# Block products of one group accumulated in shared PSUM banks, in the MLP's first product

## Chip, cores and metric

One Trainium2 chip, one of its cores. The metric is the device time of one launch, in microseconds (us). Smaller is better.

## What is computed

Two transformer blocks after each other on 1024 tokens of 1024 features, in fp32. Each block is x + mixer(norm(x)), then x + MLP(norm(x)). The mixers differ (a gated scan; a convolution beside a retention), the MLP is the same in both:

```
def sq_relu_mlp(u, w_up, w_down):
    hdn = jax.nn.relu(u @ w_up)          # [1024, 1024] @ [1024, 4096]
    return (hdn * hdn) @ w_down          # [1024, 4096] @ [4096, 1024]
```

The change is in the first of the two products, which runs once in each of the two MLPs.

## The kernel before

A fp32 product is made of three matmuls on fp32r parts: each operand is split into a high part (a ScalarE cast) and a low part (a VectorE subtraction), and `mm3` adds high x high, high x low and low x high in PSUM. An instruction's operands are printed here as moving operand first, then weights.

The MLP's products go by blocks of two by two, with seven block products in place of eight (Winograd's form). With A of the weights and B of the tokens:

```
S1 = A21 + A22, S2 = S1 - A11, S3 = A11 - A21, S4 = A12 - S2
T1 = B12 - B11, T2 = B22 - T1, T3 = B22 - B12, T4 = B21 - T2
U2 = A11 B11 + S2 T2, U3 = U2 + S3 T3
C11 = A11 B11 + A12 B21, C12 = U2 + S1 T1 + S4 B22, C21 = U3 + A22 T4, C22 = U3 + S1 T1
```

P1 is A11 B11, P2 A12 B21, P3 S4 B22, P4 A22 T4, P5 S1 T1, P6 S2 T2, P7 S3 T3. One **group** is these seven products for 256 hidden features: each is 12 matmuls (4 tiles of the contracted half, 3 parts) into a [128, 512] tile, which fills one PSUM bank. The first product of an MLP has 16 groups (0 to 15 below). The four blocks C11 (emitted as row 0, half 0), C12 (0, 1), C22 (1, 1) and C21 (1, 0) then pass max with 0 and the norm's factor `rb` (VectorE, L1155) and a square (ScalarE, L1156), and go to DRAM as blocks of the second product. Features of groups 14 and 15 are also cast and stored split (L1117, L1120).

PSUM has two pools of four banks, `acc` (called `accb()`) and `ps2` (called `bank()`). Each product takes a fresh bank. VectorE and ScalarE add up and evacuate as the products end: per group one ScalarE copy (P1, L1166) and seven VectorE additions (L1152 four times, L1173, L1175, L1179).

Order of work: each engine runs its own instructions strictly as the program emits them, and waits on semaphores for the others. Everything beside the products is planned by hand in ticks. A tick comes after each product: `tick()` first emits what is planned for this point, and only then come the copies and additions of the product just issued. Planned for the ticks are loads, the sums and splits of the next group's weight blocks (`W1_AT = (0, 3, 4, 4, 4, 4)`: full blocks at tick 0, f sums at 3, the rest at 4; L787 casts, L788 subtractions, L819 to L825 sums of which GpSimd does one), and in the last groups the splits of hidden features for the second product (L180, L181).

Group 0 is special. The last tile of its tokens is made just before it (`project`, L972 to L1000), its T sums and splits are still running while its first products run, and the norm's statistics are folded in: `rest` (split of T3, T4) at tick 0, two times eight tiny matmuls L291 (`stats_a`, `stats_b`) at ticks 2 and 3, a chain of small VectorE instructions for the root (L246 to L252), spread and turned by matmuls L305 at tick 5, and copied to `rb` by ScalarE (L1018).

Of the kernel before, what the change touches and what calls it, by code (L numbers as in the profile page):

```python
# [35 lines left out]
# Ticks (two a product of eight) between a product and each step of the side work that is planned with it.  # L36
# [17 lines left out]
# The engine of each sum of blocks: V VectorE, G GpSimd.  # L54
# [7 lines left out]
# The order of the hidden eighths (but the last) in the second product; the first eighth's parts that are stored split.  # L62
# [5 lines left out]
# columns of the small per-feature constants  # L68
# [6 lines left out]
class Slots:  # L75
    """Equal SBUF tiles of [128, 1024] words, handed out and taken back as the program is emitted."""
# [21 lines left out]
class Kernel:  # L98
# [85 lines left out]
    def use(self, n=1):  # L184
        """The next n weight slabs; loads and splits run ahead of them."""
# [15 lines left out]
    def mm3(self, ps, ah, al, bh, bl, start, stop):  # L201
        mm = self.nc.tensor.matmul
        mm(ps, lhsT=ah, rhs=bh, start=start, stop=False)  # L203
        mm(ps, lhsT=ah, rhs=bl, start=False, stop=False)  # L204
        mm(ps, lhsT=al, rhs=bh, start=False, stop=stop)  # L205

    def unit(self, w, src, half):
        """One tile of outputs [128 columns of w, 512 tokens]."""
# [12 lines left out]
    def unit_b(self, ws, src, pair, ps=None):  # L221
        """Two token tiles times 256 columns of w: [128 tokens, 2, 256]."""
        if ps is None:
            ps = self.accb()
        for j in range(2):
            self.col_b(ws, src, 2 * pair + j, range(KT), ps[:, j * 256:(j + 1) * 256])
            self.tick()
        return ps
# [10 lines left out]
    def rsqrt(self, ss, n, scale, square=False, engine=None):  # L239
        """(scale * ss + eps) ** -0.5 of a small [128, n] tile, by Newton steps."""  # L240
# [20 lines left out]
    def square_in(self, xt, j, half, sqs, gain=1.0, engine=None, late=False):  # L261
        """Adds the squares of a feature tile to the running sums."""
# [22 lines left out]
    def stats(self, sqs, chunks, ps=None):  # L285
        """Sums over the features of each token of some chunks: [128 tokens, chunks]."""
# [7 lines left out]
    def spread(self, z, n):  # L294
        """[128 tokens, n] -> n diagonal matrices of 128 tokens."""
# [6 lines left out]
    def turn(self, b, n=4):  # L302
        """n diagonal matrices of 128 tokens -> PSUM [128 equal rows, 128 n tokens]."""
# [19 lines left out]
    def hgrn_scan(self, h, qf, kr, f, v):  # L323
        """Scores within a chunk by levels: blocks of one token to blocks of 64, each with the blocks after it."""
# [7 lines left out]
        def small(ps, rhs, n):  # L332
            """Keys of each 32 tokens against n of these tokens' queries: [tokens, chunks, n]."""
# [10 lines left out]
        # Two levels at once, groups of four blocks of b tokens with totals D0 to D3:  # L344
        # queries of blocks 1, 2, 3 against the block before; D1 q2, D2 q3; D1 D2 q3.
# [142 lines left out]
    def transpose7(self, src, dst, scale):  # L488
        """Per chunk [features, tokens] -> [tokens, features], all chunks but the last."""
# [12 lines left out]
    def states7(self, kt, v, s, decay):  # L502
        """s[:, c] = the state before chunk c."""
# [16 lines left out]
    def outputs(self, a3, v, qx, s):  # L520
        """Per chunk [tokens, head features]: within the chunk, and from the state before it."""
# [66 lines left out]
    def values(self, ps, pair, vs, zs):  # L588
        """[128 tokens, 2, 256] -> two heads' values, scaled per token."""
# [1129 lines left out]
```

## Time and profile before

| | |
|---|---|
| time, median of 3 runs | 2275.82 us (2274.45 to 2278.04) |
| profiled execution, first to last instruction (the span; all that the profile gives of its own time) | 2272.1 us |
| TensorE matmul busy | 2236.2 us, 98% |
| VectorE busy | 1753.2 us, 77% |
| ScalarE busy | 879.4 us, 39% |
| GpSimd busy | 404.6 us, 18% |

PE is TensorE's matmuls, DVE is VectorE, ACT ScalarE, POOL GpSimd. Matmuls are pipelined, so one's duration (0.39 us) overlaps the next; what counts is the distance of their starts, 0.227 us for 512 columns.

### The profile page before, as it was taken

The page shows a single profiled execution, that of the slowest core. Times are in us where ns is not written, and L with a number is a line of the kernel's source. Part 1 is how long each engine was busy: PE and PEld are TensorE (multiplying, and loading weights), DVE is VectorE, ACT ScalarE, POOL GpSimd, SP SyncE. Part 2 cuts the span into 40 slices and gives each one's busy share as a digit, 9 for nine tenths or more (in the row PEclk, how much of TensorE's full clock was granted, in tenths as well). Part 3 has the DMA queues.
Part 4 walks back from the last instruction along what each step waited for, and adds up shares of the span by engine and source line. Part 5 has one row for each costly group of instructions (what it writes and reads, how often), then busy time and mean ns, then how long its engine had stood idle before and what let it go on. Part 6 is the DMA issues. An engine that isn't in the chain of part 4 may idle for free.

```text
span 2272.1 us, 32892 instructions
## 1 busy us (share of the span) xinstructions
PE 2236.2 (98%) x13102; PEld 1882.1 (83%) x13102; DVE 1753.2 (77%) x2593; ACT 879.4 (39%) x1346; POOL 404.6 (18%) x381
## 2 busy tenths in 40 slices
PE   8999999999999999999999999999999999999998
PEld 7888887888888888888889888887888888888887
DVE  6756658636888888989996556885698888889996
ACT  6334433434433335434344242224533334533322
POOL 0122212101111111222210011013111111122223
PEclk9999999999999999999999999999999999999999
DMA  5001010123344448444512011112234446744442
GB/s 181 30 29 38 21 38 30 47 74 130 118 170 160 151 167 300 152 154 149 195 46 103 28 38 38 47 38 75 89 137 165 161 152 209 261 153 147 160 158 75
DMA packets 80219, 261.91 MB, mean 115 GB/s; under 512 B 8897, under 2 KB 11457, under 8 KB 80065
## 3 DMA queue, kind: packets, MB, share of 16 engines
q1 hardware_dynamic: 79488, 259.28, 33.1%
q8 instruction: 103, 1.69, 0.3%
q10 hardware_dynamic: 576, 0.52, 0.1%
q14 instruction: 52, 0.42, 0.1%
HBM read 186.37 MB, written 73.40 MB: 114 GB/s over the span
## 4 chain that ended last, share of the span: by engine, by line
PE 86%; DVE 11%; ACT 1%; issue 1%; DMA 1%; SPq 0%; DVEq 0%; ACTq 0%
PE acc L203 20%; PE acc L204 20%; PE acc L205 20%; PE ps L203 7%; PE ps L205 7%; PE ps L204 7%; PE ps L530 1%; PE ps L532 1%; PE ps L510 1%; DVE ac L386 1%; DVE r L358 1%; DVE r L355 1%; PE ps L305 1%; PE ps L560 0%; DVE lo L174 0%
## 5 line engine op out<-in xcount | busy, mean ns | idle before, releaser
L203 PE MATMUL acc<-hi,hi 128*128 128x512 f32 (+1 forms) x824 | 315.1, 382 | 1.2 <-ACT acc L1213 1.1
L204 PE MATMUL acc<-lo,hi 128*128 128x512 f32 (+1 forms) x824 | 313.9, 381 | 0.8 <-POOL lo L1484 0.8
L205 PE MATMUL acc<-hi,lo 128*128 128x512 f32 (+1 forms) x824 | 313.8, 381 | 0.0
L203 PE MATMUL acc<-uh,hi 128*128 128x512 f32 x768 | 306.2, 399 | 0.0
L204 PE MATMUL acc<-ul,hi 128*128 128x512 f32 x768 | 300.0, 391 | 0.0
L205 PE MATMUL acc<-uh,lo 128*128 128x512 f32 x768 | 299.9, 391 | 0.0
L203 PE MATMUL ps<-hi,hi 128*128 128x512 f32 x712 | 277.2, 389 | 0.0
L205 PE MATMUL ps<-hi,lo 128*128 128x512 f32 x712 | 277.0, 389 | 0.0
L204 PE MATMUL ps<-lo,hi 128*128 128x512 f32 x712 | 277.0, 389 | 0.0
L1156 ACT ACTIVATE hq<-hq 128x512 f32<-128x512 f32 x128 | 81.0, 633 | 338.0 <-DVE hq L1155 270.8
L203 PEld LDWEIGHTS acc<-hi,hi 128*128 128x128 f32 x824 | 154.9, 188 | 32.3 <-ACT acc L1213 2.0
L204 PEld LDWEIGHTS acc<-lo,hi 128*128 128x128 f32 x824 | 154.9, 188 | 31.0 <-POOL lo L1484 1.2
L205 PEld LDWEIGHTS acc<-hi,lo 128*128 128x128 f32 x824 | 154.9, 188 | 29.7
L205 PEld LDWEIGHTS acc<-uh,lo 128*128 128x128 f32 x768 | 144.6, 188 | 30.8
L203 PEld LDWEIGHTS acc<-uh,hi 128*128 128x128 f32 x768 | 144.5, 188 | 30.4 <-ACT v L595 0.2
L204 PEld LDWEIGHTS acc<-ul,hi 128*128 128x128 f32 x768 | 144.7, 188 | 28.9 <-issue 0.5
L205 PEld LDWEIGHTS ps<-hi,lo 128*128 128x128 f32 x712 | 133.6, 188 | 27.8
L204 PEld LDWEIGHTS ps<-lo,hi 128*128 128x128 f32 x712 | 133.6, 188 | 27.7
L203 PEld LDWEIGHTS ps<-hi,hi 128*128 128x128 f32 x712 | 133.6, 188 | 27.7
L180 ACT CAST hi<-h 128x1024 fp32r<-128x1024 f32 x96 | 100.2, 1053 | 134.8 <-DVE lo L181 76.5
L181 DVE TENSOR_TENSOR lo<-h,hi 128x1024 fp32r<-128x1024 f32 x96 | 121.9, 1277 | 6.5 <-ACT hi L180 6.5
L174 DVE TENSOR_TENSOR lo<-w,hi 128x1024 fp32r<-128x1024 f32 x70 | 85.0, 1221 | 49.5 <-ACT hi L173 49.5
(271 smaller groups left out, 4696.0 us busy)
## 6 DMA issues: line engine op xcount, KB each, us to landing
w<-in_w SPq DMA_DIRECT2D x202, 512.0 KB, 4.5
hf<-f SPq DMA_DIRECT2D x28, 512.0 KB, 2.6
hfull<-hq SPq DMA_DIRECT2D x28, 512.0 KB, 3.5
hg<-g SPq DMA_DIRECT2D x28, 512.0 KB, 4.0
h<-hfull SPq DMA_DIRECT2D x28, 512.0 KB, 3.8
h<-hf SPq DMA_DIRECT2D x28, 512.0 KB, 4.5
h<-hg SPq DMA_DIRECT2D x28, 512.0 KB, 3.5
xs<-x SPq DMA_DIRECT2D x16, 512.0 KB, 2.7
```

The costliest lines, as they stand in the source:

```text
L174: self.low.tensor_tensor(lo, st, hi.bitcast(F32), op=SUB)
L180: self.nc.scalar.copy(hi, src)
L181: self.low.tensor_tensor(lo, src, hi.bitcast(F32), op=SUB)
L203: mm(ps, lhsT=ah, rhs=bh, start=start, stop=False)
L204: mm(ps, lhsT=ah, rhs=bl, start=False, stop=False)
L205: mm(ps, lhsT=al, rhs=bh, start=False, stop=stop)
L305: self.nc.tensor.matmul(ps[:, :n * P], lhsT=self.cs[:, C_ONES:C_ONES + P], rhs=b[:, :n * P], start=True, stop=True)
L355: ve.tensor_tensor(rv[:, 0:3], qv[:, 1:4], dv[:, 1:4], op=MUL)
L358: ve.tensor_tensor(rv[:, 3:5], rv[:, 1:3], dv[:, 1:3].to_broadcast([P, 2, n, b]), op=MUL)
L386: ve.copy_predicated(av[:, j:], mask[:, v0:v1], pv[:, v0:v1])
L510: nc.tensor.matmul(ps[:, c * P:(c + 1) * P], lhsT=kt[:, t], rhs=v[:, t], start=True, stop=True)
L1156: nc.scalar.activation(t, t, AF.Square)
```

## The change

The first product of both MLPs calls `chain` in place of `group`; the second product still calls `group`. The order of the products becomes P1, P2, P6, P5, P7, P3, P4, and three banks serve a group. P1, P6, P7 and P4 all go into bank x, so that it holds P1, then U2, then U3, then C21. P5 and P3 go into bank y, P2 into bank z. After P1, P6, P5 and P7 ScalarE copies the sum out (`keep`). VectorE adds three pairs (C11, C22 from two copies, C12), and C21 is read from PSUM by the max instruction itself.

```
-    def mm3(self, ps, ah, al, bh, bl, start, stop):
+    def mm3(self, ps, ah, al, bh, bl, start, stop, more=False):
         mm = self.nc.tensor.matmul
-        mm(ps, lhsT=ah, rhs=bh, start=start, stop=False)
+        mm(ps, lhsT=ah, rhs=bh, start=start, stop=False, skip_group_check=more)
...
+    CHAIN = ("P1", "P2", "P6", "P5", "P7", "P3", "P4")
+    CHAIN_BANK = {"P1": "x", "P2": "z", "P6": "x", "P5": "y", "P7": "x", "P3": "y", "P4": "x"}
+    CHAIN_W_FREE = {"P2": ("k_full",), "P5": ("k_f",), "P3": ("k_g",), "P4": ("k_one",)}
+    CHAIN_B_FREE = {"P1": ("k_one",), "P3": ("k_full",), "P5": ("k_f",), "P4": ("k_g",)}
+    def chain(self, w, bs, emit, free, own=False):
+        banks, kept = {}, {}
+        def keep(name, ps):
+            t = kept[name] = self.tmp()
+            self.nc.scalar.copy(t, ps)
+        for name in self.CHAIN:
+            an, bn = self.PARTS[name]
+            b = self.CHAIN_BANK[name]
+            fresh = b not in banks
+            if fresh:
+                banks[b] = self.accb() if b == "x" or own else self.bank()
+            ps = banks[b]
+            ah, al = w[an]
+            for k, blocks in enumerate(bs):
+                c = slice(k * P, (k + 1) * P)
+                bh, bl = blocks[bn]
+                self.mm3(ps, ah[:, c], al[:, c], bh, bl, fresh and k == 0, k == len(bs) - 1,
+                         not fresh)
...
+            self.tick()
+            if name in ("P1", "P6", "P5", "P7"):
+                keep(name, ps)
+            if name == "P2":
+                emit(0, 0, ps, kept["P1"])
+            elif name == "P7":
+                emit(1, 1, kept["P7"], kept["P5"])
+            elif name == "P3":
+                emit(0, 1, ps, kept["P6"])
+            elif name == "P4":
+                emit(1, 0, ps, None)
...
-                elif (r, h) == (1, 1):
+                elif (r, h) == (0, 1):
                     self.at(HIDDEN_AT[0], first)
...
-                t = st[r][:, tk]
-                v.tensor_tensor(t, ps, other, op=ADD)
+                t = src = st[r][:, tk]
+                if other is None:
+                    src = ps
+                else:
+                    v.tensor_tensor(t, ps, other, op=ADD)
                 def finish():
-                    v.scalar_tensor_tensor(t, t, 0.0, rb[:, tk], op0=MAX, op1=MUL)
+                    v.scalar_tensor_tensor(t, src, 0.0, rb[:, tk], op0=MAX, op1=MUL)
...
-            def out(name, ps):
-                if name == "P1":
-                    st["p1"] = self.tmp()
-                    nc.scalar.copy(st["p1"], ps)
...
-                elif name == "P6":
-                    u2 = st["u2"] = self.tmp()
-                    v.tensor_tensor(u2, ps, st["p1"], op=ADD)
-                    t = self.tmp()
-                    v.tensor_tensor(t, st["P5"], u2, op=ADD)
-                    emit(0, 1, st["P3"], t)
-                elif name == "P7":
-                    u3 = st["u3"] = self.tmp()
-                    v.tensor_tensor(u3, ps, st["u2"], op=ADD)
-                    emit(1, 1, st["P5"], u3)
...
-            self.group(w, us, 0, hidden(i), free, ("P2", "P5", "P7") if i else ("P5", "P7"))
+            self.chain(w, us, hidden(i), free, i == 0)
```

TensorE in group 0 of the first MLP, where the second product (P2, bank acc_6100) ends and the third begins. Before, the third is P3, in a bank of its own:

```order
L205 MATMUL acc_6100<-hi_5835,lo_5967 128x512
L203 MATMUL acc_6100<-hi_5979,hi_5966 128x512
L204 MATMUL acc_6100<-lo_5980,hi_5966 128x512
L205 MATMUL acc_6100<-hi_5979,lo_5967 128x512
L203 MATMUL acc_6115<-hi_5517,hi_5988 128x512
L204 MATMUL acc_6115<-lo_5518,hi_5988 128x512
L205 MATMUL acc_6115<-hi_5517,lo_5989 128x512
L203 MATMUL acc_6115<-hi_5676,hi_5988 128x512
```

Of the change, at the same place, the third is P6, in bank acc_6073, in which P1 stands:

```order
L206 MATMUL acc_6100<-hi_5835,lo_5967 128x512
L204 MATMUL acc_6100<-hi_5979,hi_5966 128x512
L205 MATMUL acc_6100<-lo_5980,hi_5966 128x512
L206 MATMUL acc_6100<-hi_5979,lo_5967 128x512
L204 MATMUL acc_6073<-hi_5539,hi_5997 128x512
L205 MATMUL acc_6073<-lo_5540,hi_5997 128x512
L206 MATMUL acc_6073<-hi_5539,lo_5998 128x512
L204 MATMUL acc_6073<-hi_5698,hi_5997 128x512
```

The bank of the third product moved from a fresh one to P1's.

ScalarE in the same group, from the cast of T1 and T2's last tile (f_5983) to the copy of `rb`. Before (g_6001 holds T3 and T4, w_6090 the next group's weights, acc_6073 is P1):

```order
L787 CAST hi_6005<-f_5983 128x1024
L787 CAST hl_6009<-w_5814 128x512
L787 CAST hi_6086<-g_6001 128x1024
L787 CAST hi_6094<-w_6090 128x1024
L1166 COPY tmp_6098<-acc_6073 128x512
L787 CAST hl_6187<-w_6092 128x512
L787 CAST hi_6190<-f_6168 128x1024
L787 CAST hi_6194<-g_6184 128x1024
L1018 COPY rb_6012<-ps_6220 128x512
L1018 COPY rb_6012<-ps_6223 128x512
L1156 ACTIVATE hq_6113<-hq_6113 128x512 x2
```

Of the change (the copies L914 are, in order, of P1, P6, P5 and P7):

```order
L788 CAST hi_6005<-f_5983 128x1024
L788 CAST hl_6009<-w_5814 128x512
L788 CAST hi_6086<-g_6001 128x1024
L788 CAST hi_6094<-w_6090 128x1024
L914 COPY tmp_6098<-acc_6073 128x512
L914 COPY tmp_6132<-acc_6073 128x512
L914 COPY tmp_6172<-acc_6134 128x512
L788 CAST hl_6189<-w_6092 128x512
L788 CAST hi_6192<-f_6169 128x1024
L788 CAST hi_6196<-g_6186 128x1024
L914 COPY tmp_6204<-acc_6073 128x512
L1063 COPY rb_6012<-ps_6220 128x512
```

P1's copy kept its place behind the four casts; the copies of P6 and P5 came in behind it, and that of P7 behind the three casts of the next weights and ahead of `rb`.

ScalarE in group 15 of the first MLP, from the first block's square on. Before (h are hidden features for the second product, w, f and g its weights):

```order
L1156 ACTIVATE hq_8414<-hq_8414 128x512
L1117 CAST tmp_8418<-hq_8414 128x512
L787 CAST hl_8440<-w_8299 128x512
L180 CAST hi_8456<-h_8263 128x1024
L180 CAST hi_8460<-h_8281 128x1024
L180 CAST hi_8485<-h_8374 128x1024
L180 CAST hi_8489<-h_8376 128x1024
L787 CAST hi_8493<-f_8385 128x1024
L787 CAST hi_8497<-g_8437 128x1024
L1156 ACTIVATE hq_8414<-hq_8414 128x512
```

Of the change (the copies are of P6, P5 and P7):

```order
L1204 ACTIVATE hq_8339<-hq_8339 128x512
L1162 CAST tmp_8343<-hq_8339 128x512
L788 CAST hl_8364<-w_8231 128x512
L914 COPY tmp_8367<-acc_8286 128x512
L180 CAST hi_8382<-h_8194 128x1024
L180 CAST hi_8386<-h_8213 128x1024
L914 COPY tmp_8398<-ps_8369 128x512
L180 CAST hi_8412<-h_8299 128x1024
L180 CAST hi_8416<-h_8301 128x1024
L788 CAST hi_8420<-f_8310 128x1024
L788 CAST hi_8424<-g_8361 128x1024
L914 COPY tmp_8435<-acc_8286 128x512
```

Three copies came in between the casts, that of P7 behind all of them.

## Rows read from the trace of the kernel before

**Rows 1.** The page's head and its first part: busy time, share of the span and number of instructions of each engine.

```profile
span 2272.1 us, 32892 instructions
PE 2236.2 (98%) x13102; PEld 1882.1 (83%) x13102; DVE 1753.2 (77%) x2593; ACT 879.4 (39%) x1346; POOL 404.6 (18%) x381
```

**Rows 2.** What TensorE waited for in the whole span: us in total, times, longest. The first is in the first block's mixer, the second at the two ends of the MLPs' first products.

```profile
PE ps L381 <- DVE r L359: 17.0, 19, 2.3
...
PE acc L203 <- ACT acc L1213: 1.1, 2, 0.9
```

**Rows 3.** Busy time of the engines in groups 1 to 14 of the first and of the second MLP.

```profile
core 0: us, PE busy (x) PEld busy (x) DVE busy (x) ACT busy (x) POOL busy (x), PEclk, DMA share, GB/s
596.00:862.00 266.00, 266.00 (x1175) 220.25 (x1174) 227.35 (x306) 94.81 (x134) 40.78 (x28) 1.00 0.46 162
1658.00:1924.00 266.00, 266.00 (x1176) 220.24 (x1175) 227.23 (x307) 94.94 (x134) 40.77 (x28) 1.00 0.46 162
```

**Rows 4.** TensorE in order of time, group 0 of the first MLP (start, duration): last matmul of the second product, first of the third, eight statistics matmuls, first matmul of the fourth, the other eight, first matmul of P4.

```profile
578.64 0.39 PE L205 MATMUL acc<-hi,lo 128*128 128x512 f32 x1
578.87 0.39 PE L203 MATMUL acc<-hi,hi 128*128 128x512 f32 x1
...
581.59 0.94 PE L291 MATMUL ps<-cs,sqs 128*128 128x1 f32 x8
582.39 0.49 PE L203 MATMUL ps<-hi,hi 128*128 128x512 f32 x1
...
585.26 0.95 PE L291 MATMUL ps<-cs,sqs 128*128 128x1 f32 x8
...
592.97 0.79 PE L203 MATMUL acc<-hi,hl 128*128 128x512 f32 x1
```

**Rows 5.** ScalarE in order of time in the same group: cast of T3 and T4, of the next weights, the copy of P1, and later the first copy to `rb` (two in one row). In brackets idle time before, and what ended it.

```profile
582.54 1.06 ACT L787 CAST hi<-g 128x1024 fp32r<-128x1024 f32 x1 [0.77 <-DVE g L849]
583.50 1.04 ACT L787 CAST hi<-w 128x1024 fp32r<-128x1024 f32 x1
584.44 0.58 ACT L1166 COPY tmp<-acc 128x512 f32<-128x512 f32 x1
...
595.47 1.06 ACT L1018 COPY rb<-ps 128x512 f32<-128x512 f32 x2
```

**Rows 6.** VectorE in order of time in the same group: the addition of C11, and the first of the small instructions for the root.

```profile
587.11 0.68 DVE L1152 TENSOR_TENSOR hq<-acc,tmp 128x512 f32<-128x512 f32 x1
587.71 0.15 DVE L246 TENSOR_SCALAR ms<-ps 128x8 f32<-128x8 f32 x1
```

**Rows 7.** Group 0 of the second MLP: first matmul of the third product, and the copy of P1.

```profile
1641.06 0.39 PE L203 MATMUL acc<-hi,hi 128*128 128x512 f32 x1
...
1646.64 0.57 ACT L1166 COPY tmp<-acc 128x512 f32<-128x512 f32 x1
```

**Rows 8.** Two stretches of the first block's mixer, columns as in rows 3; PEclk is the granted clock of TensorE as a share of 2.4 GHz.

```profile
390.00:395.60 5.60, 2.37 (x74) 1.88 (x72) 5.43 (x16) 1.02 (x2) 0.00 (x0) 1.00 0.00 0
395.60:399.20 3.60, 3.60 (x19) 2.83 (x10) 2.79 (x8) 1.62 (x4) 2.25 (x2) 0.53 0.02 5
```

**Rows 9.** Group 8 of the first MLP in order of time: its first matmul; ScalarE's cast of full weights and copy of P1; VectorE's addition of C11; ScalarE's square and its casts of f and g.

```profile
729.41 0.39 PE L203 MATMUL acc<-hl,hi 128*128 128x512 f32 x1
...
732.55 0.57 ACT L1166 COPY tmp<-acc 128x512 f32<-128x512 f32 x1
...
735.12 0.69 DVE L1152 TENSOR_TENSOR hq<-ps,tmp 128x512 f32<-128x512 f32 x1 [1.15 <-PE ps L205]
...
736.62 0.63 ACT L1156 ACTIVATE hq<-hq 128x512 f32<-128x512 f32 x1 [3.50 <-issue]
...
738.92 1.05 ACT L787 CAST hi<-f 128x1024 fp32r<-128x1024 f32 x1 [1.16 <-POOL f L820]
739.87 1.05 ACT L787 CAST hi<-g 128x1024 fp32r<-128x1024 f32 x1
```

**Rows 10.** Group 15 of the first MLP in order of time: its first matmul; on ScalarE the square of group 14's last block, then of this group's first block, the casts.

```profile
862.69 0.39 PE L203 MATMUL acc<-hl,hi 128*128 128x512 f32 x1
...
864.34 0.63 ACT L1156 ACTIVATE hq<-hq 128x512 f32<-128x512 f32 x1 [0.65 <-DVE hq L1155]
...
872.54 0.63 ACT L1156 ACTIVATE hq<-hq 128x512 f32<-128x512 f32 x1 [3.58 <-DVE hq L1155]
...
873.74 0.62 ACT L787 CAST hl<-w 128x512 fp32r<-128x512 f32 x1
874.26 3.89 ACT L180 CAST hi<-h 128x1024 fp32r<-128x1024 f32 x4
878.05 1.05 ACT L787 CAST hi<-f 128x1024 fp32r<-128x1024 f32 x1
879.01 1.04 ACT L787 CAST hi<-g 128x1024 fp32r<-128x1024 f32 x1
```

**Rows 11.** After group 15: the matmul of the second product that waited for ScalarE's copy L1213, in the first and in the second MLP.

```profile
892.32 0.50 PE L203 MATMUL acc<-hi,hi 128*128 128x512 f32 x1 [0.91 <-ACT acc L1213]
...
1953.83 0.50 PE L203 MATMUL acc<-hi,hi 128*128 128x512 f32 x1 [0.22 <-ACT acc L1213]
```

**Rows 12.** Groups of equal instructions over the whole span (busy us, mean ns of one, idle before): the first copy and two of the additions of the groups, 32 groups in all.

```profile
L1175 DVE TENSOR_TENSOR tmp<-ps,tmp 128x512 f32<-128x512 f32 x32 | 22.1, 691 | 1.1
L1173 DVE TENSOR_TENSOR tmp<-acc,tmp 128x512 f32<-128x512 f32 x32 | 22.0, 688 | 12.5 <-PE acc L205 11.7
...
L1166 ACT COPY tmp<-acc 128x512 f32<-128x512 f32 x32 | 18.4, 576 | 0.0
```

More of the change, by code (lines that the diff above doesn't have):

```diff
@@ L198, in done @@
             self.slots.put(hi, lo)
-    def mm3(self, ps, ah, al, bh, bl, start, stop):
+    def mm3(self, ps, ah, al, bh, bl, start, stop, more=False):
         mm = self.nc.tensor.matmul
-        mm(ps, lhsT=ah, rhs=bh, start=start, stop=False)
-        mm(ps, lhsT=ah, rhs=bl, start=False, stop=False)
-        mm(ps, lhsT=al, rhs=bh, start=False, stop=stop)
+        mm(ps, lhsT=ah, rhs=bh, start=start, stop=False, skip_group_check=more)
+        mm(ps, lhsT=ah, rhs=bl, start=False, stop=False, skip_group_check=more)
+        mm(ps, lhsT=al, rhs=bh, start=False, stop=stop, skip_group_check=more)
     def unit(self, w, src, half):
@@ L898 @@
     B_FREE = {"P1": ("k_one",), "P3": ("k_full",), "P6": ("k_f",), "P4": ("k_g",)}
+    CHAIN = ("P1", "P2", "P6", "P5", "P7", "P3", "P4")
[20 more added lines that the diff above has]
+                         not fresh)
+            for sets, table in free:
+                for key in table.get(name, ()):
+                    for st in sets:
+                        self.slots.put(*st[key])
+            self.tick()
[9 more added lines that the diff above has]
+                emit(1, 0, ps, None)
     def group(self, w, bs, c0, out, free, second=("P2", "P5", "P7")):
@@ L1161, in emit @@
                     waiting.pop(0)()
-            def out(name, ps):
-                if name == "P1":
-                    st["p1"] = self.tmp()
-                    nc.scalar.copy(st["p1"], ps)
-                elif name in ("P2", "P3", "P5"):
-                    st[name] = ps
-                    if name == "P2":
-                        emit(0, 0, ps, st["p1"])
-                elif name == "P6":
-                    u2 = st["u2"] = self.tmp()
-                    v.tensor_tensor(u2, ps, st["p1"], op=ADD)
-                    t = self.tmp()
-                    v.tensor_tensor(t, st["P5"], u2, op=ADD)
-                    emit(0, 1, st["P3"], t)
-                elif name == "P7":
-                    u3 = st["u3"] = self.tmp()
-                    v.tensor_tensor(u3, ps, st["u2"], op=ADD)
-                    emit(1, 1, st["P5"], u3)
-                else:
-                    emit(1, 0, ps, st["u3"])
-            return out
+            return emit
         self.at(0, lambda: self.load_to(base + 4))
@@ L1188, in mlp @@
             w = w_next
-            free = [([w], self.W_FREE)]
+            free = [([w], self.CHAIN_W_FREE)]
             w_next = self.prep_w(base + 2 * i + 2, *((W1_AT, W1_BY) if i < 15 else (W2_FIRST_AT, W2_FIRST_BY)))
@@ L1194, in mlp @@
             if i == 15:
-                free.append((us, self.B_FREE))
+                free.append((us, self.CHAIN_B_FREE))
                 self.at(RESIDUAL_AT[0], lambda: [load_x(g) for g in range(2)])
                 self.at(RESIDUAL_AT[1], lambda: [load_x(g) for g in range(2, 4)])
-            self.group(w, us, 0, hidden(i), free, ("P2", "P5", "P7") if i else ("P5", "P7"))
+            self.chain(w, us, hidden(i), free, i == 0)
         S.put(rb)
```

## Prediction, written before the changed kernel ran

> **What bounds the kernel now.** I read the page's head first: TensorE's matmuls are busy 98% of a span of 2272.1 us, VectorE 77%, ScalarE 39% [rows 1]. So time can be won only where TensorE stands still, and it is lost wherever it is made to. Next the table of waits, for TensorE alone: the longest line, 17.0 us, lies in the first mixer, which the change doesn't touch. In the MLPs' first products there is one line that matters, 1.1 us in all, at their ends [rows 2]. Then the busy time by stretch: in groups 1 to 14 TensorE is busy 266.00 us out of 266.00, in both MLPs, at the full granted clock (1.00, the 2.4 GHz level); 1176 matmuls in 266 us are 0.226 us each, which is their distance, so a product of 12 takes 2.72 us and a group 19.04 us [rows 3]. VectorE is busy 227 us of these 266 and ScalarE 95: VectorE is heavily loaded, but nothing in TensorE's stream waits for it.
>
> **What is removed.** Four VectorE additions in each of 32 groups, 0.69 us each [rows 12]: 4 x 32 x 0.69 = 88 us of VectorE's time. Worth on the path: nothing in groups 1 to 14, since TensorE doesn't wait there. It can give back only the wait at the end: there TensorE waited 0.91 and 0.22 us for a ScalarE copy [rows 11] that stood behind squares, which stood behind VectorE's additions. With its slower first matmul (0.50 for 0.39, twice) this is 0.91 + 0.22 + 2 x 0.11, about 1.4 us. VectorE is four additions (2.8 us) earlier there, so I count all of it: -1.4.
>
> The matmuls stay the same in number and shape, and so do DMAs; the loads' ticks don't move, so SP and GpSimd keep their queues. The step `first` moves from the emission of C22 to that of C12, which is the sixth product's in both orders, so it comes in the same tick. C21's max now reads PSUM: no row shows that form; between an addition out of PSUM at 0.69 and the slowest max in the trace (some 1.8) it stays on VectorE, which waits for nobody's sake here. I take 0.7 and no effect.
>
> **What is added.** Three ScalarE copies a group, 0.58 us each [rows 12], 55 us in all, on an engine with 171 of 266 us free [rows 3]. More important is who waits. Before, each product had its own bank; now TensorE may not write P6 into bank x before ScalarE has copied P1 out of it, nor P7 before P6's copy, P3 before P5's, P4 before P7's. Between a product's end and the next write to its bank lies one other product, 2.72 us. A copy takes 0.58 and starts about 0.28 behind the product's end (the fifth product's start to VectorE's addition, below), so 1.9 us are left for whatever stands ahead of it on ScalarE, which works strictly in order. So each copy's neighbours in the queue have to be walked through, and there are three kinds of group.
>
> **Groups 1 to 14.** In group 8 P1 starts at 729.41, so P2 ends at 734.85 and the addition of C11 follows at 735.12, 0.27 later. P1's copy ran at 732.55 and ended at 733.12; P6 would start at 734.85: free by 1.7. The square of C11 is done at 737.25, P6 ends at 737.57, its copy at about 738.4, and P7 starts at 740.29: free by 1.9. P5's copy ends at 741.15, P3 starts at 743.01. The three casts of the next weights now queue behind P5's copy: 741.1 + 0.5 + 0.95 + 0.95 = 743.5, behind which P7's copy (P7 ends at 743.01) runs to 744.1; P4 starts at 745.73, free by 1.6 [rows 9]. Cost nothing; the cover is that one product of 2.72 us, and a cast more ahead of a copy would use most of it.
>
> **Group 0.** Here the queue is another. P1's copy stands behind the cast of T3 and T4 (which waits 0.77 for VectorE) and the cast of the next weights; in the order of both kernels this place is the same. In the trace it ran at 584.44 and ended at 585.02 [rows 5], whereas TensorE began its third product at 578.87 [rows 4]. Before, nobody but a late addition on VectorE (587.11 [rows 6]) needed it. Now the third product is P6, in P1's bank: TensorE stands from 578.87 to 585.02, **6.15 us**. In the second MLP the same two rows give 1647.21 - 1641.06 = 6.15 [rows 7].
>
> The delay doesn't stay at that. What is late next: P6 ends at 587.74, the first eight statistics matmuls take 0.80, P5 2.87, the second eight 0.95 (all from [rows 4]): 592.4, and with 0.1 to VectorE the small instructions for the root start at 592.5, for 587.71 before [rows 6]: 4.8 late. Behind them, on VectorE, stand the sums of the next weights; behind those GpSimd's; behind that ScalarE's casts of f and g; and behind these casts, where the first copy to `rb` ran at 595.47 [rows 5], stands now P7's copy. It ends at 595.47 + 4.8 + 0.58 = 600.85. P4 waits for it, and started at 592.97 before: **7.9 us** late in all (P3 and the matmuls L305 are done at about 599.1, so some 1.8 of it is a second stand). Both MLPs: 15.8. In group 1 the queue is back in step: its copies have the room of group 8 within 0.4.
>
> **The clock after the stand.** In the first mixer TensorE worked 2.37 of 5.60 us in small matmuls, and then the granted clock was 0.53 for 3.60 us, the 1.2 GHz level [rows 8]. At that level full matmuls stood 0.43 apart; ten intervals took 3.75 us for 2.27, so 1.5 lost. In group 0 TensorE will do nothing at all for 6.15. I take a fall of the same length in both MLPs: 3.0; the bounds are 0 and, if the second stand brings another, 6.0. The Trainium skill's page "TensorE: Matmul & The Clock Gate" (What's actually happening) says that the half-rate clock is the default and that only activity lifts it, which would give the fall and 2297. The trace agrees in that one place; that the clock stays up, as it does over the mixer's shorter waits, would give 2294.
>
> **Group 15.** The casts of hidden features L180 stand between the copies. Before, ScalarE's square of C11 ran at 872.54 behind a long VectorE queue, then 873.74 to 874.26 a cast, four casts, two casts [rows 10]. One addition fewer ahead makes the square 0.7 earlier. P6's copy follows the cast, at 873.56 to 874.14, but P7 would start at 862.69 + 4 x 2.72 = 873.57: 0.6 late. Then four casts at 0.97 with P5's copy (0.5) between, casts of f and g at 0.95: P7's copy runs from 880.3 to 880.9, P4 would start at 879.01: **1.9 us** late in all. VectorE's subtractions and loads are the same as before in the second MLP, so twice: 3.8. Bounds 0 (if the casts find room elsewhere) and 2.4 each.
>
> **Sum.** 15.8 + 3.0 + 3.8 - 1.4 = +21.2 us on a span of 2272.1. The median of the runs is 2275.82, 3.7 above the span, which I carry over: **2297 us**, 0.93% slower.
>
> **Why it can't just skip the wait.** The Trainium skill's page "PSUM — Partial Sum Buffer" (PSUM bank collisions raise a hardware error) says that the chip doesn't arbitrate between a matmul's write and another engine's read of the same bank and raises an error, so that semaphores have to keep them apart. It speaks against copying a bank in the middle of its chain: by it the wait is there and the sum 2297, without it 2274. No row of the trace before shows such a bank; the built order of the change has the copy as the event for which P6's first matmul waits.
>
> **The rivals.** First, the stands without the fall of the clock: 2294. For it: only one place in the span shows a fall after waits, against: nowhere else does TensorE idle this long in the middle. Chance 0.25, and 0.58 for the forecast. Second, the delay in group 0 is the first stand alone, because P7's copy finds VectorE's chain early enough: 12.3 in place of 15.8, no fall: 2275.8 + 12.3 + 3.8 - 1.4 = 2290.5. Against it: VectorE stands idle at 587.8 for the statistics, which come behind P5 in TensorE's order. Chance 0.10. Third, the copies are hidden in group 0 too, so that only the end's 1.4 is won: 2274, no change; it asks that P1's copy come 6 us earlier in ScalarE's queue, which the order denies. Chance 0.03.
>
> On the other side: matmuls get closer together. 512 columns at 2.4 GHz are 0.213 us, and the rows show 0.226 to 0.227; if the 0.0135 came from VectorE's reading of PSUM beside the matmuls, fewer readings and banks could give 2 x 16 x 84 x 0.0135 = 36 us, and 2297 - 36 = 2261, faster. It decides once about 0.0097 of the 0.0135 go (26 us of 36). Against it: the distance is the same in group 8 where VectorE stands idle for 1.15 us [rows 9] as over all the groups [rows 3]. Chance 0.02. The last 0.02 is a stall that I have missed, above the range.
>
> **Range and chances.** Below, the second rival less a small error: 2288; above, a second fall of the clock, group 15 at its bound, and one more us in each group 1 if its copies lack their room: 2297 + 3 + 1 + 2: 2303. The measurement can tell some 0.2% (4.5 us) from no change. Slower by more: 0.58 + 0.25 + 0.10 + 0.02 = 0.95; within: 0.03; faster: 0.02.
>
> **What would show it.** TensorE's waits in the changed kernel should have a new line on ScalarE's copies L914: in group 0 some 6.2 and then 1.8 us, in group 15 some 0.6 and 1.3, each twice, near 20 us together; no such wait in groups 1 to 14; the granted clock near 0.5 for some 3.5 us from 585 on; the wait for the second product's copy gone. VectorE's busy time should fall by 80 to 90 us, ScalarE's rise by 55. I am wrong if P1's copy in group 0 runs before 580, if TensorE's wait list has no L914, or if the matmuls' distance moves from 0.227.

## Result and the profile after

The changed kernel takes 2298.23 us (median of 4 runs, 2297.47 to 2299.01) beside 2276.11 for the kernel before (2274.45 to 2278.04): slower by 22.1 us. The ratio is 1.0100, with a 95% interval of 1.0086 to 1.0114. The forecast was 2297, in a range of 2288 to 2303, so time and direction came out as forecast. The experiments below show that one reason given in it was incomplete all the same.

The page's head and first part of the changed kernel, which answer to [rows 1], and the first lines of what TensorE waited for (us in total, times, longest), which answer to [rows 2]:

```profile
span 2297.2 us, 32805 instructions
PE 2243.5 (98%) x13102; PEld 1886.5 (82%) x13102; DVE 1656.5 (72%) x2465; ACT 933.6 (41%) x1442; POOL 404.9 (18%) x381
```

```profile
PE acc L204 <- ACT tmp L914: 18.6, 7, 6.1
PE ps L382 <- DVE r L360: 17.1, 19, 2.3
```

VectorE lost 97 us of work, more than the 80 to 90 that were expected (the max instructions take 692 ns on the mean, where L1155 took 828 in the kernel before; why that was so, no run asks). ScalarE gained 54. And there is one new line at the top: TensorE waits seven times for the copies L914, 18.6 us in all. The wait for the second product's copy is gone. So where are the seven? First the dense part, groups 1 to 14 of each MLP, as busy time by stretch (columns as in [rows 3]):

```profile
604.50:871.00 266.50, 266.50 (x1177) 220.73 (x1177) 179.89 (x244) 117.49 (x175) 40.77 (x28) 1.00 0.46 163
1679.40:1945.90 266.50, 266.50 (x1177) 220.66 (x1177) 179.89 (x244) 117.52 (x175) 40.45 (x28) 1.00 0.46 163
```

TensorE has no hole there, at the same distance of matmuls as before, although VectorE has only 180 us to do where it had 227. All seven waits are in groups 0 and 15. TensorE in order of time (start, duration; in brackets idle time and what ended it): third product and last product of group 0, first MLP; third product of group 0, second MLP; P7 and P4 of group 15, first MLP; P7 of group 15, second MLP:

```profile
577.44 0.39 PE L206 MATMUL acc<-hi,lo 128*128 128x512 f32 x1
583.88 0.80 PE L204 MATMUL acc<-hi,hi 128*128 128x512 f32 x1 [6.05 <-ACT tmp L914]
...
601.68 0.50 PE L204 MATMUL acc<-hi,hl 128*128 128x512 f32 x1 [1.13 <-ACT tmp L914]
...
1658.45 0.80 PE L204 MATMUL acc<-hi,hi 128*128 128x512 f32 x1 [6.05 <-ACT tmp L914]
...
882.88 0.50 PE L204 MATMUL acc<-hi,hi 128*128 128x512 f32 x1 [0.75 <-ACT tmp L914]
...
889.54 0.50 PE L204 MATMUL acc<-hi,hl 128*128 128x512 f32 x1 [0.93 <-ACT tmp L914]
...
1959.57 0.50 PE L204 MATMUL acc<-hi,hi 128*128 128x512 f32 x1 [2.52 <-ACT tmp L914]
```

From start to start the third product of group 0 is 583.88 - 577.44 - 0.23 = 6.21 us late. ScalarE in the same group, in order of time, shows why, and why P4 is late as well. The first three rows stand in the order of [rows 5], at the same distance from the group's start; the last three are the casts of f and g and behind them P7's copy:

```profile
581.35 1.05 ACT L788 CAST hi<-g 128x1024 fp32r<-128x1024 f32 x1 [0.77 <-DVE g L850]
582.30 1.04 ACT L788 CAST hi<-w 128x1024 fp32r<-128x1024 f32 x1
583.25 0.58 ACT L914 COPY tmp<-acc 128x512 f32<-128x512 f32 x1
...
599.15 1.05 ACT L788 CAST hi<-f 128x1024 fp32r<-128x1024 f32 x1 [5.57 <-POOL f L821]
600.10 1.04 ACT L788 CAST hi<-g 128x1024 fp32r<-128x1024 f32 x1
601.05 0.58 ACT L914 COPY tmp<-acc 128x512 f32<-128x512 f32 x1
```

And the clock, as busy time by stretch: the stand, the matmuls behind it, and the same behind P7 in group 15 of the second MLP:

```profile
577.60:583.80 6.20, 0.23 (x2) 0.00 (x0) 6.20 (x11) 4.92 (x6) 0.00 (x0) 0.79 0.59 203
583.80:588.20 4.40, 4.32 (x10) 3.42 (x11) 2.81 (x3) 0.03 (x1) 0.00 (x0) 0.52 0.41 167
...
1959.50:1963.70 4.20, 4.13 (x11) 3.28 (x12) 3.44 (x4) 4.20 (x7) 0.00 (x0) 0.59 0.97 281
```

Behind the stand the granted clock was 0.52, near the 1.2 GHz level: ten intervals from 583.88 to 588.20 took 4.32 us in place of 2.27, the time of ten at the distance of [rows 3].

The books, from the starts of groups: group 0 lasts from 572.23 to 604.54, 32.31 us, where it was 22.70; in the second MLP 32.65 for 22.71. So +9.6 and +9.9. Group 15 gives +2.3 in the first MLP (2.0 of it the two stands, the rest the first matmuls behind them), and +4.4 in the second, 2.7 of it the stand and 1.7 the clock. With the forecast's 1.4 for the wait that is gone this is 24.8, and the two profiled spans differ by 25.1.

### The profile page after: what moved, and what is told of

Read it like the earlier page. It is cut to its first block, busy times and chain, and to the rows that moved or that the text cites. A ratio compares the mean times of both kernels' runs of the same rounds, so it can differ in the third digit from the quotient of the medians.

```text
span 2297.2 us, 32805 instructions
## 1 busy us (share of the span) xinstructions
PE 2243.5 (98%) x13102; PEld 1886.5 (82%) x13102; DVE 1656.5 (72%) x2465; ACT 933.6 (41%) x1442; POOL 404.9 (18%) x381
## 4 chain that ended last, share of the span: by engine, by line
PE 85%; DVE 11%; ACT 2%; issue 1%; DMA 1%; SPq 0%; POOL 0%; DVEq 0%; POOLq 0%; ACTq 0%
PE acc L204 20%; PE acc L205 20%; PE acc L206 20%; PE ps L204 7%; PE ps L205 7%; PE ps L206 7%; PE ps L531 1%; PE ps L533 1%; PE ps L511 1%; DVE ac L387 1%; DVE r L359 1%; DVE r L356 1%; ACT hi L788 0%; PE ps L561 0%; DVE lo L174 0%
## 5 line engine op out<-in xcount | busy, mean ns | idle before, releaser
L204 PE MATMUL acc<-hi,hi 128*128 128x512 f32 (+1 forms) x840 | 325.0, 387 | 15.5 <-ACT tmp L914 15.4
L205 PE MATMUL acc<-lo,hi 128*128 128x512 f32 (+1 forms) x840 | 323.0, 385 | 0.7 <-POOL lo L1511 0.7
L206 PE MATMUL acc<-hi,lo 128*128 128x512 f32 (+1 forms) x840 | 322.6, 384 | 0.0
L205 PE MATMUL ps<-lo,hi 128*128 128x512 f32 x696 | 270.8, 389 | 0.0
L204 PE MATMUL ps<-hi,hi 128*128 128x512 f32 x696 | 270.8, 389 | 0.0
L206 PE MATMUL ps<-hi,lo 128*128 128x512 f32 x696 | 270.7, 389 | 0.0
L204 PEld LDWEIGHTS acc<-hi,hi 128*128 128x128 f32 x840 | 159.6, 190 | 48.4 <-ACT tmp L914 17.0
L205 PEld LDWEIGHTS acc<-lo,hi 128*128 128x128 f32 x840 | 159.9, 190 | 32.0 <-POOL lo L1511 1.2
L206 PEld LDWEIGHTS acc<-hi,lo 128*128 128x128 f32 x840 | 159.7, 190 | 31.1
```

The lines of the kernel that those rows point to most:

```text
L204: mm(ps, lhsT=ah, rhs=bh, start=start, stop=False, skip_group_check=more)
L205: mm(ps, lhsT=ah, rhs=bl, start=False, stop=False, skip_group_check=more)
L206: mm(ps, lhsT=al, rhs=bh, start=False, stop=stop, skip_group_check=more)
```

## Experiments

Each kernel is the changed one with the edit shown; `...` stands for lines of an edit that are not shown. "Against before" is the median less that of the kernel before on the same chip.

### Group 0 put back; groups 0 and 15 put back

```
-            self.chain(w, us, hidden(i), free, i == 0)
+            if i in OLD:      # (0,) in g0_old, (0, 15) in ends_old
+                self.group(w, us, 0, hidden(i), free, ...)
+            else:
+                self.chain(w, us, hidden(i), free, i == 0)
...
```

The lines not shown bring back, for these groups, the additions `out` and the table of freed tiles of the kernel before.

> Group 0 of each MLP goes the old way (seven banks, old order, VectorE's seven additions); groups 1 to 15 stay chained. My theory: group 0 takes 22.7 us again in place of the 32.3 and 32.6 that the changed kernel's trace shows, so the time falls by 9.6 + 9.9 = 19.5 us, from 2298.2 to 2278.7; what is left above the kernel before is group 15. Rival (the delay comes from shared banks in every group, and is only paid where the queue runs empty): less than half of it goes, 2290 or more.

> Groups 0 and 15 of each MLP go the old way, groups 1 to 14 stay chained (28 of 32 groups). My theory: nothing is paid or won in groups 1 to 14, so 2276, the time before within 0.1%, with VectorE busy some 77 us less than before. Rival (the shared bank costs a little in every group, or fewer readings of PSUM by VectorE let the matmuls come closer): 0.1 us a product would be 20 us, 2296 or 2256.

Neither came out as my theory had it (ends_old lies between its theory's 2276 and its rival's 2296). g0_old took 2292.5 us, 16.8 against before (ratio 1.0072, 1.0058 to 1.0086); ends_old 2288.0, 12.2 against before (1.0051, 1.0039 to 1.0064). The rival's number for g0_old, 2290 or more, held; its reason, a delay in every group, is ruled out by from4 below. Group 0 does last 22.7 us again in both. But a stand came up that was in no trace yet, here in ends_old at the third product of group 1, with ScalarE's rows ahead of it:

```profile
606.43 0.79 PE L205 MATMUL acc<-hi,hi 128*128 128x512 f32 x1 [4.67 <-ACT tmp L915]
```

```profile
601.17 1.83 ACT L1205 ACTIVATE hq<-hq 128x512 f32<-128x512 f32 x3 [4.61 <-DVE hq L1204]
604.33 0.63 ACT L1205 ACTIVATE hq<-hq 128x512 f32<-128x512 f32 x1 [1.32 <-DVE hq L1204]
604.86 1.03 ACT L789 CAST hi<-w 128x1024 fp32r<-128x1024 f32 x1
605.80 0.58 ACT L915 COPY tmp<-acc 128x512 f32<-128x512 f32 x1
```

P1's copy of group 1 stands behind group 0's squares, and these wait for VectorE, which runs late after group 0. The kernel before has the same lateness, and its trace had shown it: the copy of P1 in groups 1, 2 and 3 of the kernel before, on ScalarE, where TensorE doesn't wait for it:

```profile
605.81 0.57 ACT L1166 COPY tmp<-acc 128x512 f32<-128x512 f32 x1
...
622.71 0.58 ACT L1166 COPY tmp<-acc 128x512 f32<-128x512 f32 x1
...
639.62 0.57 ACT L1166 COPY tmp<-acc 128x512 f32<-128x512 f32 x1
```

They are 16.9 us apart, while a group takes 19.04: the lateness shrinks by 2.14 us a group. The third product of group 1 is due at 596.13 + 5.44 = 601.57, and 605.81 + 0.57 - 601.57 = 4.81; the stand of ends_old is 4.83 (its gap of 5.06 from start to start, less 0.23). With the fall of the clock behind it group 1 lasts 25.9 and 26.0 us in ends_old, 25.6 and 26.8 in g0_old, in place of 19.04. In the changed kernel the stand of group 0 had given VectorE time to catch up, and VectorE had four additions fewer to do there; group 1 showed no wait. How much each of the two gave, no run separates. New theory: the chain pays for the lateness once, in whichever group it begins, at the price that is left there.

### Chain from group 2 on; chain from group 4 on

```
+OLD = (0, 1, 15)          # from2
+OLD = (0, 1, 2, 3, 15)    # from4
```

> Chain in groups 2 to 14 only; groups 0, 1 and 15 go the old way. With group 0 alone put back, a stand of 4.83 us came up in group 1. My theory: VectorE and ScalarE run late after group 0 and catch up 2.14 us a group (their period is 16.9 for 19.04 of a group: P1's copy starts at 605.81, 622.71 and 639.62 in the trace of before), so the first chained group pays what is left of the lateness. Chained from group 2: 622.71 + 0.58 against a third product due at 615.15 + 5.44 = 620.59, a stand of 2.7 in each MLP, and 0 to 1.6 each for the clock: 2276 + 5.4 to 8.6, 2281 to 2285. Rival (the first chained group always pays the same, a price of the change of order itself): 2276 + 2 x (4.8 + 1.6) = 2289, with the stand still near 4.8.

> Chain in groups 4 to 14 only, 11 of 16; the others go the old way. My theory: by group 4 the lateness of VectorE and ScalarE is used up (4.8, 2.7, 0.5, none), so no stand on ScalarE's copies is left in TensorE's waits, and the time is that of before, 2276 within 0.1%, with some 61 us less of VectorE. Rival (the shared banks cost in every group, if little): 2278 to 2285. Rival (fewer VectorE readings of PSUM let matmuls come closer): under 2272.

from2 took 2283.4 us, 7.3 against before (1.0034, 1.0023 to 1.0046); from4 2275.0, 1.2 below before (0.9995, 0.9986 to 1.0004: no difference). What TensorE waited for: the line on L915 of from2, then the longest line of from4 and the first part of its page; and the stand of from2 in group 2:

```profile
PE acc L205 <- ACT tmp L915: 5.1, 2, 2.6
```

```profile
PE ps L383 <- DVE r L361: 17.0, 19, 2.3
```

```profile
PE 2239.3 (98%) x13102; PEld 1885.6 (83%) x13102; DVE 1684.0 (74%) x2505; ACT 915.9 (40%) x1412; POOL 402.9 (18%) x381
```

```profile
623.66 0.50 PE L205 MATMUL acc<-hi,hi 128*128 128x512 f32 x1 [2.60 <-ACT tmp L915]
```

The stand is 2.76 us from start to start (2.68 in the second MLP) where 2.7 was expected; behind it the clock fell in both MLPs, 1.7 us each. The rival, a stand near 4.8 wherever the chain begins, fell. With 11 of 16 groups chained, all past the lateness, no wait on the copies L915 is left in from4's list. VectorE does 69 us less in from4 than in the kernel before (1684.0 for 1753.2), and the time is the same within the interval. That settles the dense groups: nothing is paid there, and no more is won than the wait for the second product's copy [rows 11], 1.1 us in all. It has no line in from4's list, nor in those of ends_old and g15_old, although group 15 goes the old way in all three.

### The clock

```
+            if own and name == "P6":
+                spare = self.bank()
+                for k in range(24):
+                    self.nc.tensor.matmul(spare, lhsT=w["A11"][0][:, :P], rhs=bs[0]["B11"][0], ...)
```

> All groups chained; in group 0 of each MLP 24 matmuls of 128x512 into a spare bank, which nobody reads, stand between P2 and P6 (24 x 0.227 = 5.4 us of a stand of 6.2). They replace no work; the output is the same. My theory: the stand stays as long as it was, since P1's copy ends where it did, but TensorE keeps its granted clock, so the 1.6 to 1.9 us of matmuls 0.43 apart behind it go, in both MLPs: 2298.2 - 3.5 = 2294.7, the rows behind the stand at 0.227. Rival (the fall of the clock has nothing to do with TensorE standing still): 2298 with the same slow rows.

warm took 2294.4 us, 18.3 against before (1.0080, 1.0065 to 1.0095). TensorE at the stand, and the busy time by stretch of the stand and what follows (the same two stretches as above):

```profile
579.93 5.60 PE L927 MATMUL ps<-hl,hi 128*128 128x512 f32 x24
586.14 0.50 PE L204 MATMUL acc<-hi,hi 128*128 128x512 f32 x1 [0.61 <-ACT tmp L914]
```

```profile
579.90:586.10 6.20, 5.64 (x25) 4.32 (x23) 6.20 (x11) 4.92 (x6) 0.00 (x0) 1.00 0.66 222
586.10:590.50 4.40, 4.36 (x23) 3.77 (x24) 2.76 (x3) 0.58 (x1) 0.00 (x0) 1.00 0.46 140
```

P6 starts as late as in the change, but at a granted clock of 1.00, so the rival, the same slow rows, fell. Group 0 lasts 30.42 and 30.47 us for 32.31 and 32.65. So a fall behind this stand costs 1.9 to 2.2 us of group 0, 4.1 in both MLPs. The medians give 22.1 - 18.3 = 3.8 us, which agrees, but they alone would not show it: the two intervals overlap (1.0086 to 1.0114 and 1.0065 to 1.0095).

### The order alone

```
+            if own and name == "P6":
+                banks[b] = self.accb()
+                fresh = True
...
```

The lines not shown add P1 on VectorE to the copies of P6 and P7 and to the last block, in group 0 alone, so the order is not quite the only difference.

> The order of the change in all groups, but in group 0 P6 starts a bank of its own, so that nobody waits for P1's copy there; VectorE adds P1 to three sums in group 0. My theory: the new order alone costs as well, since P6 is third and needs T2 of the last token tile, whose low part VectorE ends at 583.05 in the changed kernel's trace, while P6's tenth to twelfth matmul come up at 579.7: a stand of about 3.3 behind the tenth. So 5.1 us of the first stand and the clock's fall go, not all, in each MLP: 2298.2 - 10.2 = 2288, up to 2291 if the clock falls. Rival (only the bank costs, the order is free): the first stand is gone, 2298.2 - 2 x 7.8 = 2282.6 or less, unless a stand comes up in group 1.

p6_fresh took 2287.7 us, 13.4 against before (1.0065, 1.0047 to 1.0083). With a bank of its own P6 still waits in group 0, for its operands:

```profile
578.49 0.50 PE L204 MATMUL acc<-hi,hi 128*128 128x512 f32 x1 [0.72 <-ACT hi L788]
578.83 0.40 PE L205 MATMUL acc<-lo,hi 128*128 128x512 f32 x1
580.10 0.51 PE L206 MATMUL acc<-hi,lo 128*128 128x512 f32 x1 [0.88 <-DVE lo L789]
...
583.04 0.79 PE L205 MATMUL acc<-lo,hi 128*128 128x512 f32 x1
```

The new order asks for S2 and T2 third. S2's high part comes at 578.5 and its low part at 580.05, each some 1 us too late, and T2's only 0.2 late at 583.04: my figure of one stand of 3.3 was in the wrong place. That the time came to 2288 all the same is luck: the clock, for which I had allowed up to 3 us more, fell here too. The rival (the order is free, 2282.6 or less) fell. P7's copy is late as in the change (P4 starts 1.72 behind the matmul before it). Group 0 lasts 28.1 and 27.9 us: of the 9.6 to 9.9 that the change adds, 5.2 to 5.4 remain when P1's bank is not in the way. 1.3 of them are the stand behind P7's copy, the rest P6's late operands and the clock.

### The copy's place in ScalarE's queue

```
+            ahead = True     # all_early, and best (with group 0 put back)
+            ahead = own and name in ("P1", "P7")      # g0_early
+            if ahead and name in ("P1", "P6", "P5", "P7"):
+                keep(name, ps)
             self.tick()
-            if name in ("P1", "P6", "P5", "P7"):
+            if not ahead and name in ("P1", "P6", "P5", "P7"):
                 keep(name, ps)
```

> All groups chained, but each ScalarE copy is emitted ahead of the tick of its product, not behind it. My theory: in group 0 P1's copy still stands behind two casts of T and weight blocks that end at 580.5 in the trace, so it ends at 581.1 and P6 starts 2.7 earlier; P7's copy passes the casts of the next weights, and the second stand (1.3) is gone; in group 15 the copy of P7 passes four casts, some 1.5 less. Twice 2.7 + 1.3 + 1.5 = 11: 2287, and 2284 if the clock stays up after the shorter stand. Rival (the place of the copy in ScalarE's queue doesn't matter, the hand-over of the bank itself costs): 2298, no change.

> Group 0 the old way, groups 1 to 15 chained with each copy ahead of its product's tick. My theory: group 0 costs nothing (-19.5), group 15 loses most of its stands (-3 of the 6.5 that both show), the wait at the end of the groups stays away: 2275.5, the kernel before within 0.1%. Rival (VectorE's 80 us less work is worth something once no copy is late): clearly below the kernel before, 2270 or less.

> All groups chained, as in the change; only in group 0 the copies of P1 and P7 are emitted ahead of their product's tick. My theory, from the run with all copies ahead: group 0 takes 27.8 us for 32.3 (first stand 3.4 for 6.2, second gone), no new stand in group 1, group 15 as in the change: 2298.2 - 2 x 4.6 = 2289. Rival (what group 0 saves comes up as a stand in group 1, as when group 0 was put back): 2292 or more, with a stand on L914 in group 1.

g0_early took 2287.2 us, 12.9 against before (1.0060, 1.0044 to 1.0076), all_early 2291.8, 16.0 against before (1.0074, 1.0060 to 1.0088), best 2296.8, 21.0 against before (1.0086, 1.0071 to 1.0101). In group 0 the place is what counts, so the rival, the hand-over of the bank itself, fell. P6's first matmul and P1's copy of g0_early:

```profile
584.32 0.50 PE L204 MATMUL acc<-hi,hi 128*128 128x512 f32 x1 [3.27 <-ACT tmp L914]
```

```profile
583.17 0.61 ACT L788 CAST hl<-w 128x512 fp32r<-128x512 f32 x1
583.69 0.57 ACT L914 COPY tmp<-acc 128x512 f32<-128x512 f32 x1
584.56 1.05 ACT L788 CAST hi<-g 128x1024 fp32r<-128x1024 f32 x1 [0.29 <-DVE g L850]
```

Two casts passed, 2.8 us of the stand gone (3.4 left), and the second stand gone too. In the first MLP the clock stayed up behind the shorter stand (group 0 lasts 26.3 us), in the second it fell (27.7). No stand came up in group 1, as the theory for g0_early had it.

best missed by 21 us, and all_early by 5: putting every copy ahead made group 15 worse. It lasts 24.1 us in both kernels and both MLPs, 5.0 more than the 19.04 before; 3.1 of that are the stands and 1.7 the clock. (The profiled execution of all_early took 2296.4, 4.6 above its median, so the clock may have fallen less often in its others; that of best lies near its median.) ScalarE in group 14 of all_early, then in group 15, with P7's first matmul of group 15:

```profile
864.87 0.59 ACT L914 COPY tmp<-acc 128x512 f32<-128x512 f32 x1 [2.13 <-PE acc L206]
865.35 0.62 ACT L788 CAST hl<-w 128x512 fp32r<-128x512 f32 x1
865.87 1.05 ACT L788 CAST hi<-f 128x1024 fp32r<-128x1024 f32 x1
...
882.44 0.63 ACT L1207 ACTIVATE hq<-hq 128x512 f32<-128x512 f32 x1 [3.65 <-DVE hq L1206]
883.11 0.62 ACT L1165 CAST tmp<-hq 128x512 fp32r<-128x512 f32 x1
883.63 0.58 ACT L914 COPY tmp<-acc 128x512 f32<-128x512 f32 x1
```

```profile
884.26 0.50 PE L204 MATMUL acc<-hi,hi 128*128 128x512 f32 x1 [2.53 <-ACT tmp L914]
```

A copy moved ahead waits for its product's end, and holds the casts behind it. The cast of f starts 14.8 us into group 14, where it was 12.1 in the changed kernel; VectorE's subtractions stand behind that cast, the square of C11 in group 15 waits for VectorE (3.65, above), and P6's copy stands behind that square. best also has the stand of group 1 (3.9 and 3.8 us), which g0_old and ends_old show. Its expectation was written before their results were known.

### Group 15 put back

```
+OLD = (15,)
```

> Groups 0 to 14 chained as in the change, group 15 of both MLPs the old way. My theory: the stands of group 15 go (1.0 + 1.1 with the first MLP, 1 to 2.7 with the second, 0 to 1.6 for the clock), and the short wait at the end of the groups comes back (0.4 to 1.1 in each): 2298.2 - 4.5 to 6.5 + 1.4, 2293 to 2295. Rival (group 15's stands are covered, as group 0's covered those of group 1): 2298.

g15_old took 2294.5 us, 20.2 against before (1.0092, 1.0076 to 1.0108). In its trace group 15 lasts 19.04 us again in both MLPs, so the stands do go and the rival fell. By the medians it is 1.9 less than the 22.1 of the change: below the 3.1 to 5.1 that I expected, and the two intervals overlap for the most part, so the medians leave the size open. Beside ends_old, g0_old, which differs in group 15 alone, gives 2292.5 - 2288.0 = 4.5 on one chip. The traces of four other kernels that chain group 15 as the change does (g0_old, warm, p6_fresh, g0_early) show stands of 1.9 to 2.3 us in each MLP and no fall of the clock; group 15 lasts 2.2 to 2.6 us longer there, 4.4 to 4.8 in both MLPs. I had set the end's 1.4 against that, but that wait does not come back with the old group 15. So some 4.5 us is the size on which these traces and the pair g0_old and ends_old agree.

### How large a copy's room is

```
+MORE = 6
...
-            self.nc.scalar.copy(t, ps)
+            for _ in range(1 + (MORE if name == "P7" and more else 0)):
+                self.nc.scalar.copy(t, ps)
...
```

`more` is true in groups 1 to 14.

> All groups chained; in groups 1 to 14 the copy of P7 is made seven times over (six more ScalarE copies, 0.48 us apart: 2.86 us). In the trace of the changed kernel P7's copy in group 8 ends at 752.39 and P4 is due at 754.14, 1.75 us of room. My theory: a copy costs nothing while it fits the product between, so 2.86 - 1.75 = 1.1 us a group is paid, 28 times: 31 us, 2329. Rival (the room is larger, since what follows P7 on ScalarE takes up the rest): 2298, no change. Rival (every copy is paid in full): 28 x 2.86 = 80, 2378.

slack6 took 2374.1 us, 76 more than the change (98.0 against before, 1.0429, 1.0414 to 1.0443): much more than the 31 expected. ScalarE and P4's first matmul in group 7:

```profile
751.09 4.29 ACT L916 COPY tmp<-acc 128x512 f32<-128x512 f32 x7
```

```profile
755.43 0.50 PE L205 MATMUL acc<-hi,hl 128*128 128x512 f32 x1 [1.84 <-ACT tmp L916]
```

The room is as expected, the price of a copy was not: seven copies into the same tile take 4.29 us, 0.62 from start to start, not 0.48. Six more are 3.71, less 1.75 of room 1.96, and the stand is 2.23 - 0.23 = 2.0. The first matmul behind a stand takes 0.1 more than its 0.23; so a group lasts 21.18 us, and 28 x 2.14 = 60. The rest is for the most part the clock: behind nine of these 28 equal stands it fell, at some 1.6 each. The rival that every copy is paid in full named a number near to this (80), but not this reason: P4 waits 2.0 us, not 3.7.

## Why the prediction was right, and where it wasn't

**Group 0, first stand: right.** 6.15 us forecast, 6.21 and 6.21 measured, worked out from two rows of the trace before, the third product's start in [rows 4] and the end of P1's copy in [rows 5]. The Trainium skill's page "PSUM — Partial Sum Buffer" (PSUM bank collisions raise a hardware error) asks for just this wait; the seven waits on L914 agree. That the page speaks against copying a bank in the middle of its chain, as I put it, holds for a copy without that wait only: the changed kernel makes four in each group with it. What I put at nothing was the new order: P6 comes third now, and its operands are not ready then. In the changed kernel this stays hidden behind P1's copy; p6_fresh shows it, two stands of some 1 us.

**Group 0, second stand: right.** Forecast were "some 1.8", with 7.9 in all; measured were 1.3, behind a P6 that the low clock had made longer: 32.31 - 22.70 = 9.6, against 7.9 + 1.5 = 9.4. The difference of 0.5 is a slip in my sum: behind the 592.4 P7 and P3 take 2 x 2.72 and the four matmuls L305 0.43 each, which is 599.5 and not 599.1, and 600.85 - 599.5 is 1.3 to 1.4. The cause is the place of P7's copy behind the casts: in g0_early, with the copy ahead of them, the stand is gone, and in p6_fresh, where the first stand is short, it is as long as in the change.

**The clock: mechanism right, size a little small.** 1.5 was forecast for each MLP, warm took back 1.9 and 2.2. The Trainium skill's page "TensorE: Matmul & The Clock Gate" (What's actually happening) says that activity lifts the clock; warm agrees, at a granted clock of 1.00 behind matmuls whose result nobody reads. The rival "no fall" (0.25) fell.

**Group 15: right in kind, too small.** 1.9 us each was forecast; the first MLP shows stands of 2.0, the second one of 2.7 and a fall of the clock of 1.7, for which the forecast had no term here. I had written that loads' ticks and SP's queue stay, and they do, but not their times. A store in SP's queue waits for VectorE's low part L1165, and that for the casts behind the new copies, so the load of a hidden eighth (hf) was issued 1.5 us ahead of group 15 where it was 2.7 ahead; in the second MLP it landed late, and ScalarE's cast waited 2.23 us for it:

```profile
1952.88 1.06 ACT L180 CAST hi<-h 128x1024 fp32r<-128x1024 f32 x1 [2.23 <-DMA h<-hf]
```

In warm and g0_early that wait was 0.85 and 0.68, and in g0_old and p6_fresh there was none, so this term has spread.

**Groups 1 to 14: right, for too short a reason.** No wait, and no change in the matmuls' distance, so the rival on the other side fell as well. But "in group 1 the queue is back in step" held only because group 0 was chained too: it stood still, and VectorE had less to do in it. With group 0 put back, 4.8 us came up in group 1. The step that I left out: VectorE and ScalarE leave group 0 about 5 us late in the kernel before, which its separate banks hid, and the chain has to pay for that somewhere. It doesn't change the forecast; it does change what an undo of group 0 is worth: 22.1 - 16.8 = 5.3 us by the medians, and not 19.5.

**The sum.** The forecast was +21.2; the medians differ by 22.1. That they come so close is in part luck, for by the traces the terms add up to more: 19.5 for group 0 where 18.8 was forecast, 6.7 for group 15 in place of 3.8, 24.8 with the end's 1.4 taken off, and the two profiled spans differ by 25.1. Part of that is the late load. Part is the 3.7 that I carried over from the span to the median, which mixed two executions: in the later runs each execution of the kernel before lies 2.1 to 2.2 above its own span, and the changed kernel's lie 1.8 above theirs (2299.0 for 2297.2). So the profiled execution of the kernel before was some 1.5 below its median. The rivals in which only the first stand remains, or none, fell with the second stand's rows.

## What to carry to other kernels

When products share a bank, the slack that separate banks gave to the evacuating engine is gone: look for the latest evacuation in each stage of the old trace, not in the steady stage alone, and compare it with the time at which the bank's next write is due; the difference is the stand. Such a stand pays off lateness that the next stages would otherwise have shown, so undoing it locally uncovers the next one, and the new form is free only from the stage on where the engines are back in step (here group 4 of 16 or sooner; by the rows of the kernel before 0.5 us would be left in group 3, which no run tried). In a strict queue neither end is safe: a copy behind the casts makes the next product late, and one ahead of them makes the casts wait for its product.

## What the runs showed of the hardware beyond that

- Behind equal stands the clock falls in some and not in others. In slack6 nine of 28 stands of 2.0 us were followed by matmuls 0.43 us apart. Behind the same waits of the first mixer the kernel before has a granted clock of 0.53 [rows 8], and the changed kernel, at the same place, 1.00:

```profile
395.90:399.60 3.70, 3.70 (x35) 3.04 (x23) 2.88 (x8) 1.62 (x3) 2.26 (x2) 1.00 0.02 4
```

The stands of 6.2 us in group 0 were followed by a fall six times out of six (twice each in the changed kernel, slack6 and g15_old), and in warm, where the hole was filled, not once. The stands of 4.8 us in g0_old and ends_old were followed by one four times out of four, those of 2.7 in from2 twice out of two.

- ScalarE's copies into one tile, one behind the other, start 0.62 us apart (4.29 us for seven, above), though one alone takes 0.58 and a cast behind a copy starts 0.48 after it (864.87 and 865.35, above).
- The max that reads PSUM directly takes 0.69 us, as much as the one that reads SBUF in the same kernel. These are its two groups in the changed kernel (busy us, mean ns):

```profile
L1203 DVE SCALAR_TENSOR_TENSOR hq<-hq,rb 128x512 f32<-128x512 f32 x96 | 66.1, 692 | 3.1
...
L1203 DVE SCALAR_TENSOR_TENSOR hq<-acc,rb 128x512 f32<-128x512 f32 x32 | 22.1, 691 | 25.9 <-PE acc L206 25.9
```
